# Seven products for each masked table, u ahead of the last quarter of Z, and norms in four parts

## The chip, the cores and the metric

The kernel runs on one core of one Trainium2 chip. The time is that of one execution on the device in microseconds (us). Five engines work on their own queues and meet at semaphores: TensorE (PE in the profile; PEld is its weight loads), VectorE (DVE), ScalarE (ACT), GpSimd (POOL) and SyncE (SP), which here issues all DMA transfers in one queue.

## The reference

One encoder layer is applied to two sequences, a prompt of 256 tokens and a sample of 2048, of width 1024. Half of the layer is attention in a window of a grid of 64 columns, the other half a two-dimensional Fourier transform:

```python
def encoder_layer(x, w_in, rpb, w_fourier, b_fourier, g_pre, g_na, g_f, w_out, g_post):
    h = rms_norm(x, g_pre)
    proj = h @ w_in
    q, k, v, z_a, u_f, z_f = jnp.split(proj, [...], axis=-1)     # six parts of 512
    y_a = neighbourhood_attention(q, k, v, rpb)
    y_f = fourier_mix(u_f, w_fourier, b_fourier)
    mixed = jnp.concatenate([rms_norm(y_a, g_na) * jax.nn.silu(z_a),
                             rms_norm(y_f, g_f) * jax.nn.silu(z_f)], axis=-1)
    out = mixed @ w_out
    return x + rms_norm(out, g_post)
```

The attention has 8 heads of 64. A query sees 8 rows by 16 columns of keys around it; what is outside counts as minus infinity, and a table `rpb` of relative positions is added:

```python
        logits = jnp.einsum('bjqhd,bijkhd->bhjqik', q_blk, k_slab).astype(jnp.float32) * scale
        bias = bias_table[:, row_off[None, None, :, None], col_off[:, :, None, :]]
        logits = jnp.where(valid[:, :, None, :], logits + bias, NEG_INF)
        p = jax.nn.softmax(logits.reshape(shp[:4] + (kr * K_SLAB_COLS,)), axis=-1).reshape(shp)
```

The Fourier half takes the real part of a transform over the positions and over the 64 features of each of 8 groups, and multiplies by a 512 x 512 matrix:

```python
    spec = jnp.fft.fft2(ug, axes=(1, 3), norm='ortho')
    mixed = spec.real.reshape(b, s, F_WIDTH).astype(u.dtype)
    return mixed @ w_f + b_f
```

## The kernel before, in words

Everything is in 32 bits. A product of matrices is made of three passes over operands split into a high and a low part (`mm3`, L159: lines L160 to L162 of the profile), so each operand is first copied by ACT to its high part and the rest is taken by DVE or POOL. PE's order is that of the program. In the long first part and in the last one the order of ACT, DVE, POOL and SP is that of the program too (`tc.manual_schedule(engines=MAN)`, L506 to L784 and from L1165); between L784 and L1165 a planner orders these four by its own estimates of when things are ready.

**Projections, L506 to L781.** First v and u. u goes through the first step of the Fourier transform and lies in DRAM as `ZD` (sample) and `uD` (prompt). Then the prompt's z, k and q. Then, from L686, the sample's z, k and q: 16 groups (`i`), 8 for each half of the sample's columns (`sg`), of seven products each (`j`, L722), which replace eight plain ones. One product is 12 matmuls into one of five PSUM buffers (`mmt`, L209); DVE, or ACT for the first, adds it to what it belongs to (`comb` L711, `add` L763, ACT L765), which frees the buffer. While group i is multiplied, the weights of group i+1 are combined by POOL (`w_sums`, L440) and split (`a_split`, L454 and L455), and those of group i+2 are loaded at j = 3 (`w_load`, L225). The results go to DRAM (L717, L719). The seven transformed inputs of the second half of the sample come back from DRAM through `b_get` and `b_split` (L419, L424).

**Masked tables, L479 to L503.** In the second half of the groups, and so beside these products, the bias tables of the 8 heads of the sample are masked. `t_load` (L483) takes two of 16 buffers of 8 KB per partition ("k8") and loads the raw table; `t_mask(x, 0)` puts the column mask on DVE (L489); `t_mask` with 1, 2 and 3 puts three row masks on POOL (L493), one for each kind of row; `t_store` writes two tables (L499, L500), then the third (L502). The other 14 k8 buffers hold the split inputs, so a table waits for the buffers of the one before it. The step in the code by which a table goes on is one product, and a table has six of them, from product 0 of the second half on.

**Fourier, L788 to L906.** Four quarters of `ZD` are loaded (`load_z`, L794, four transfers each) with the transform's matrices (L225), then u of the prompt (`up`, L825) and its matrix (`f256`, L823), then three more. The first two take buffers of the pool `gp`, which come free as products are done; `f256`, `up` and the rest lie in memory that the projections' pools held. For each quarter `gq` and five column blocks `c` PE makes `pab`; in the third quarter it also makes `pup` from `up` after each block (all L850). Then come the products with the Fourier weights (`ppq`, L888).

**Attention and output, from L1041.** 36 groups of a head pair and a part of the rows; iteration `k` of the loop at L1374 makes the scores of group k, the transposes and products with v of group k-1 (`transp` L1310, `pv` L1326) and half of a tile of the Fourier half's output (`f_mm`, L1256). The Fourier half's norms are sums over `sqs`, made by PE against a column of ones (`f_norm`, L1293, tile `pfn`), then a few small operations on ACT and DVE (`rsq_ops`); `f_evac(k)` needs the norm of tile k // 2. The pool of `sqs` is closed after the last of them (`pq_.close()`). The attention half has the same for its own norms (`a_norm`, L1300, tile `pna`).

Of the kernel before, what the change touches and what calls it, by code (L numbers as in the profile page):

```python
# [164 lines left out]
def build(tc, A, O):  # L165
# [54 lines left out]
    def gt(shape, dtype, name):  # L220
        return gp.tile(shape, dtype, tag="g", name=name)
# [143 lines left out]
    def n_load(x):  # L365
        if type(x) is tuple:
            nq[x] = k8(F32, "nx")
            nc.sync.dma_start(nq[x], A["xq"][0, x[0], x[1]])
            return
        nx = [k8(F32, "nx") for kh in range(2)]  # L370
        for kh in range(2):
            for b in range(2):
                nq[x, kh, b] = nx[kh][:, 2 * b:2 * b + 2]
                nc.sync.dma_start(nq[x, kh, b], A["xq"][1, kh, b][:, 2 * x:2 * x + 2])
# [55 lines left out]
    def pair(i):  # L430
        return i if i < 8 else 15 - i
# [3 lines left out]
    def w_load(i):  # L435
        wr[i] = [load(BS, A["wz"][2 * pair(i) + x], "wr") for x in range(2)]

    def w_sums(i, last=False):
        h = lambda f, k: wr[i][f][:, 4 * k:4 * k + 4]
        T2 = lambda o, i, j, op: nc.gpsimd.tensor_tensor(out=o, in0=i, in1=j, op=op)  # L440
        if last:
            T2(h(0, 1), h(0, 1), wo[i][:, 1], ALU.subtract)
            return
        wo[i] = gt([128, 2, 4, 128], F32, "ws")
        T2(wo[i][:, 0], h(1, 0), h(1, 1), ALU.add)
        T2(wo[i][:, 1], wo[i][:, 0], h(0, 0), ALU.subtract)
        T2(h(1, 0), h(0, 0), h(1, 0), ALU.subtract)
# [48 lines left out]
    def t_store(x, q):  # L496
        pr, h = divmod(x, 2)
        if q == 0:
            nc.sync.dma_start(tD[0][pr][:, h], mt[1][:, :880])  # L499
            nc.sync.dma_start(tD[2][pr][:, h], mt[1][:, 880:1840])  # L500
        else:
            nc.sync.dma_start(tD[1][pr][:, h], mt[0][:, :1200])  # L502
            mt.clear()  # L503
# [145 lines left out]
    for b in range(16):  # L649
# [25 lines left out]
        if kind % 2:  # L675
            i, d = p, o
        else:
            i = p.rearrange("p (b r c) -> p b r c", b=2, c=32)
# [7 lines left out]
    for i in range(16):  # L686
        sg, pr = divmod(i, 8)
        kind, blk = divmod(2 * pair(i), 4)
        o = [st.tile([128, 1024], F32, tag="f", name="f", bufs=3) for x in range(2)]
        uu = {}  # L690

        def e_(name):
            uu[name] = st.tile([128, 512], F32, tag="e", name=name, bufs=6)
            return uu[name]

        def dst(f, b):
            if kind % 2 == 0:
                return o[f].rearrange("p (x b c) -> p b x c", b=2, c=32)[:, b]
            if kind == 1:
                return o[f].rearrange("p (a b j) -> p b a j", b=2, j=256)[:, b]  # L700
            return o[f].rearrange("p (y b x c) -> p y x b c", y=2, b=2, c=16)[:, b]

        def src(a):
            if kind % 2 == 0:
                return a.rearrange("p (x c) -> p x c", c=32)
            if kind == 1:
                return a.rearrange("p (a j) -> p a j", j=256)
            return a.rearrange("p (x b c) -> p x b c", b=2, c=16)

        def comb(f, b, u, p, op=ALU.add):  # L710
            nc.vector.tensor_tensor(out=dst(f, b), in0=src(uu[u]), in1=src(p), op=op)  # L711

        def store(f):
            ts = slice(TP + 1024 * sg, TP + 1024 * sg + 1024)
            if kind < 2:
                silu_[0] = nc.scalar.activation(o[f], o[f], AF.Silu)
                nc.sync.dma_start(zD[kind, (blk + f) * 128:(blk + f) * 128 + 128, ts], o[f])  # L717
            else:
                nc.sync.dma_start((kD if kind == 2 else qD)[blk + f, :, ts], o[f])  # L719

        silu_ = [None]
        for j in range(7):  # L722
            if i == 7:
                aop[8, j] = aop[7, j]
            elif i < 15:
                if j == 0 and i != 8:
                    w_sums(i + 1)
                a_split(i + 1, j)
            if i == 7 and j == 1:
                w_sums(9)  # L730
            if j == 3 and i < 14 and i != 7:
                w_load(i + 2 + (i == 6))
            if sg == 0:
                x, y = divmod(7 * (pr - 1) + j, 14)
                if x in (0, 1):
                    if y == 0:
                        n_load(x)
                    elif 3 <= y < 7:
                        n_scale(x, *divmod(y - 3, 2))
                    elif 7 <= y < 12:  # L740
                        n_diff(x, y - 7)
                if pr == 6 and j in (0, 3):
                    (b_split if j else b_get)(0)
                if pr == 7 and j:
                    b_get(j)
                    if j > 2:
                        b_split(j - 2)
            if i == 8 and j < 2:
                b_split(j + 5)
            if sg:  # L750
                x, y = divmod(7 * pr + j, 6)
                if x < 8 and y == 0:
                    t_load(x)
                for q in {2: (0, 1), 3: (2,), 4: (3,)}.get(y, ()) if x < 8 else ():
                    t_mask(x, q)
                if x < 8 and y > 3:
                    t_store(x, y - 4)
            p = mmt(512)
            at = aop[i, j]
            bh, bl = bnew[sg, j]  # L760
            for k in range(4):
                mm3(nc, p, at[:, 0, k], at[:, 1, k], bh[:, k], bl[:, k], k == 0, k == 3)
            add = lambda o, u: nc.vector.tensor_tensor(out=e_(o), in0=uu[u], in1=p, op=ALU.add)  # L763
            if j == 0:
                nc.scalar.copy(e_("u0"), p)  # L765
            elif j == 1:
                comb(0, 0, "u0", p)
            elif j == 2:
                add("u2", "u0")
            elif j == 3:  # L770
                add("u4", "u2")
            elif j == 4:
                comb(1, 1, "u4", p)
                add("u3", "u2")
            elif j == 5:
                comb(1, 0, "u3", p, ALU.subtract)
                store(1)
            else:
                comb(0, 1, "u4", p)
                store(0)  # L780
        if kind < 2:  # L781
            silu = silu_[0]
# [5 lines left out]
    def load_z(gq):  # L788
        r = []
        for j in range(2):  # L790
            z = gt([128, 2, 512], F32, "zg")
            for i in range(2):
                g8 = (gq * 4 + 2 * j + i) * 8
                nc.sync.dma_start(z[:, i, :], ZD[g8:g8 + 8].rearrange("o n c -> (o n) c"))  # L794
            r += [z[:, 0, :], z[:, 1, :]]
        return r
# [4 lines left out]
    zgs = [load_z(0)]  # L801
    d2 = [load_d(0)]
    zgs.append(load_z(1))
    d2.append(load_d(1))
    zgs += [load_z(2), load_z(3)]
    ph.close()


# [14 lines left out]
    nc.sync.dma_start(f256, A["f256"])  # L823
    up = sm.tile([128, 2, 512], F32, name="up")
    nc.sync.dma_start(up, uD.rearrange("(t p) c -> p t c", p=128))  # L825
    cs2 = sm.tile([128, 2, 64], F32, name="cs2")
    nc.sync.dma_start(cs2, A["cs"])
    c32 = sm.tile([128, 4, 96], F32, name="c32")
# [461 lines left out]
    def f_norm(ts):  # L1290
        p = ps.tile([128, 18], F32, tag="c", name="pfn", bufs=1)
        for t in ts:
            nc.tensor.matmul(p[:, t:t + 1], sqs[:, t * 128:t * 128 + 128], ones, start=True, stop=True)  # L1293
        ts = slice(ts[0], ts[-1] + 1)
        rsq_ops(invf[:, ts], p[:, ts], ts.stop - ts.start, 1.0 / 512)
# [23 lines left out]
    def pv(g):  # L1319
# [28 lines left out]
        if R is None or hc:  # L1348
            nc.sync.dma_start(yD[0, pr, :, ts], y)

    WO = []

    YSQ = {2: [(Y2, 256, 512), (Y2, 512, 1024)], 3: [(Y, 256, 512), (Y2, 1024, 1664)], 4: [(Y2, 1664, 2304)],
           5: [(Y, 512, 1110)], 6: [(Y, 1110, 1708)], 7: [(Y, 1708, 2304)]}
    ftiles[0]["h"], ftiles[0]["l"] = y0h
# [18 lines left out]
    for k in range(2, len(G) + 1):  # L1374
        pr, i = divmod(k, 9)
# [17 lines left out]
        if 24 <= k < 32:  # L1393
            y = k - 24
            nc.sync.dma_start(WO[y % 2][:, y // 2].bitcast(F32), woD[0, y % 2, y // 2])
        x = k // 2 + 1
# [12 lines left out]
        if g:  # L1409
            exps(g, 0, 1)  # L1410
            bias_max(g, 1, 1)
            exps(g, 1, 0)
            f_mm(k, range(6))
            soft(g, 0)
            exps(g, 1, 1)
            if k in (4, 8):
                f_norm(range(2, 4) if k == 4 else range(4, 18))
        else:
            a_mm(atiles[0], 0, range(6))
            a_norm(atiles[:14])  # L1420
# [9 lines left out]
        run_later()  # L1430
        for v, x0, x1 in YSQ.get(k, []):
            nc.scalar.activation(v[:, x0:x1], v[:, x0:x1], AF.Square)
# [14 lines left out]
            f_evac(k)  # L1447
        if f:
            pv(f)
        if k == 8:  # L1450
            pq_.close()
        if k + 1 < len(G):
            prep_v(G[k + 1])
# [4 lines left out]
        if 32 <= k < 36:  # L1458
            x, d = k - 32, atiles[k - 32]
# [123 lines left out]
```

## Time and profile before

| | us |
|---|---|
| median of 3 runs | 1015.97 (1010.14 to 1021.81) |
| profiled execution | 1016.24 |
| its span, first to last instruction | 1014.4 |
| PE busy | 994.8 |
| DVE busy | 698.2 |
| ACT busy | 472.8 |
| POOL busy | 434.9 |

The groups of seven products run from 268 to 578 us of the span, with the tables from 424 on; the Fourier stage runs from 578 to 642, attention from there to 910, and the output's last part to the end. PE's mean granted clock is 0.990 of full speed.

In the rows of the profile "L160" is a line of the kernel, "mm<-xh,wa" the tile written and the tiles read, "x12" a count, and "[2.50 <-DMA mt<-tr]" idle time of the engine ahead of the row and what ended it. Rows of the timeline begin with the start and the duration in us. "SPq" is an issue of a DMA transfer, not the transfer. The matmuls are pipelined, so a matmul's duration is longer than the distance to the next one.

### The profile page before, as it was taken

The numbers are of one execution on the slowest core, as the hardware profiler recorded it, in microseconds if no ns is written. First come the engines' busy times: TensorE is split into PE (matmuls) and PEld (weight loads), VectorE is DVE, ScalarE is ACT, GpSimd is POOL, SyncE is SP. The second block draws the span as 40 slices with busy tenths as digits, with TensorE's granted clock in tenths as the row PEclk, the third lists the DMA queues.
The fourth block names the chain that finished last, engine by engine and source line by source line (L and its number), as shares of the span: only waits on it lengthen the run. The fifth ranks groups of instructions, "written<-read, shape, count | busy, mean of one in ns | idle before, by whom it ended". The sixth has DMA issues, their size and how long they took to land. (4 is left out here: it accounts for less than half of the span.)

```text
span 1014.4 us, 16956 instructions
## 1 busy us (share of the span) xinstructions
PE 994.8 (98%) x5828; PEld 824.7 (81%) x5828; DVE 698.2 (69%) x1287; ACT 472.8 (47%) x1022; POOL 434.9 (43%) x401
## 2 busy tenths in 40 slices
PE   7999999999999999999999999999999999999997
PEld 6778888889988888888778878878787787888886
DVE  7777637668777884896667634775565655648997
ACT  6554434256524322522123245576666676645443
POOL 2300000000526363575576113466668586633444
PEclk9999999999999999999999979999999999999999
DMA  7467798777446664866456897588678889869993
GB/s 253 140 183 221 219 322 302 265 248 242 148 170 248 233 225 171 342 215 238 168 214 231 300 327 280 195 267 265 193 248 267 277 283 289 273 222 332 345 338 131
DMA packets 153254, 249.33 MB, mean 246 GB/s; under 512 B 14033, under 2 KB 99345, under 8 KB 150609
## 3 DMA queue, kind: packets, MB, share of 16 engines
q1 hardware_dynamic: 153168, 248.26, 72.2%
q8 instruction: 46, 0.75, 0.3%
q14 instruction: 40, 0.32, 0.1%
HBM read 160.13 MB, written 88.08 MB: 245 GB/s over the span
## 5 line engine op out<-in xcount | busy, mean ns | idle before, releaser
L160 PE MATMUL mm<-xh,wa 128*128 128x512 f32 x448 | 175.3, 391 | 2.8 <-DVE u L763 2.2
L161 PE MATMUL mm<-xl,wa 128*128 128x512 f32 x448 | 175.2, 391 | 0.0
L162 PE MATMUL mm<-xh,wa 128*128 128x512 f32 x448 | 175.0, 391 | 0.0
L160 PE MATMUL mm<-wc,xh 128*128 128x512 f32 x288 | 113.7, 395 | 5.2 <-ACT xh L270 5.2
L161 PE MATMUL mm<-wc,xh 128*128 128x512 f32 x288 | 113.7, 395 | 1.1 <-DVE wc L248 1.0
L162 PE MATMUL mm<-wc,xl 128*128 128x512 f32 x288 | 113.0, 392 | 0.0
L1039 POOL TENSOR_SCALAR w<-w,m 128x480 f32<-128x480 f32 (+6 forms) x136 | 83.2, 625 | 64.1 <-DVE m L1036 52.3
L160 PEld LDWEIGHTS mm<-xh,wa 128*128 128x128 f32 x448 | 84.5, 189 | 21.2 <-issue 3.6
L161 PEld LDWEIGHTS mm<-xl,wa 128*128 128x128 f32 x448 | 84.5, 189 | 17.6
L162 PEld LDWEIGHTS mm<-xh,wa 128*128 128x128 f32 x448 | 84.6, 189 | 17.5
L1256 PE MATMUL po<-wo,yh 128*128 128x512 f32 x272 | 91.3, 417 | 0.0
L455 DVE TENSOR_TENSOR wa<-wr,wa 128x512 fp32r<-128x512 f32 x60 | 71.6, 1203 | 25.5 <-ACT wa L454 25.1
L1256 PE MATMUL po<-w,yh 128*128 128x512 f32 x280 | 86.7, 391 | 0.0
L1032 ACT ACTIVATE w<-w,m 128x480 f32<-128x480 f32 (+6 forms) x136 | 79.3, 586 | 15.3 <-DVE m L1027 15.2
L440 POOL TENSOR_TENSOR ws<-wr 128x512 f32<-128x512 f32 x15 | 22.0, 1464 | 129.5 <-DMA wr<-wz 97.2
L271 POOL TENSOR_TENSOR xl<-xr,xh 128x1024 fp32r<-128x1024 f32 x5 | 12.2, 2450 | 136.1 <-ACT xh L270 72.4
L1027 DVE CUSTOM_DVE_ANT_1 w<-s,tb 128x360 f32<-128x360 f32 (+5 forms) x124 | 62.5, 541 | 9.1 <-PE s L1005 8.5
L160 PEld LDWEIGHTS mm<-wc,xh 128*128 128x128 f32 x288 | 54.6, 189 | 16.9 <-ACT xh L270 5.2
L454 ACT CAST wa<-wr 128x512 fp32r<-128x512 f32 x60 | 36.0, 617 | 68.1 <-POOL wr L440 16.2
L493 POOL TENSOR_TENSOR mt<-mt,rmask 128x880 f32<-128x880 f32 (+2 forms) x24 | 51.1, 2138 | 37.1 <-DVE mt L489 34.6
L161 PEld LDWEIGHTS mm<-wc,xh 128*128 128x128 f32 x288 | 54.6, 190 | 14.1 <-DVE wc L248 2.8
L162 PEld LDWEIGHTS mm<-wc,xl 128*128 128x128 f32 x288 | 54.7, 190 | 11.2
(234 smaller groups left out, 2310.0 us busy)
## 6 DMA issues: line engine op xcount, KB each, us to landing
wr<-wz SPq DMA_DIRECT2D x46, 512.0 KB
oD<-ofs SPq DMA_DIRECT2D x18, 512.0 KB
of<-oD SPq DMA_DIRECT2D x18, 512.0 KB
yr<-yD SPq DMA_DIRECT2D x34, 256.0 KB
woD<-wo SPq DMA_DIRECT2D x16, 512.0 KB
zD<-f SPq DMA_DIRECT2D x16, 512.0 KB
xr<-xs SPq DMA_DIRECT2D x15, 512.0 KB
vD<-vo SPq DMA_DIRECT2D x112, 64.0 KB
```

The source lines that it names most:

```text
L160: nc.tensor.matmul(out, lh, rh, start=first, stop=False)
L161: nc.tensor.matmul(out, lh, rl, start=False, stop=False)
L162: nc.tensor.matmul(out, ll, rh, start=False, stop=last)
L271: (nc.gpsimd if c in XP else nc.vector).tensor_tensor(out=l, in0=xs[c][:, ks], in1=h.bitcast(F32), op=ALU.subtract)
L440: T2 = lambda o, i, j, op: nc.gpsimd.tensor_tensor(out=o, in0=i, in1=j, op=op)
L454: nc.scalar.copy(o[:, 0], src)
L455: nc.vector.tensor_tensor(out=o[:, 1], in0=src, in1=o[:, 0].bitcast(F32), op=ALU.subtract)
L493: nc.gpsimd.tensor_tensor(out=o, in0=i, in1=rmask[:, m0:m0 + n].unsqueeze(2).to_broadcast([128, n, 80]), op=ALU.add)
L1027: nc.vector.tensor_tensor_reduce(out=rows(g["w"][b][:, h, :n], w), in0=rows(g["s"][2 * b + h][:, :n], w), in1=tv, scale=1.0, scalar=3.0e38 ...
L1032: nc.scalar.activation(w, w, AF.Exp, bias=m[:, h:h + 1], scale=-1.0, accum_out=m[:, 2 + h:3 + h])
L1039: nc.gpsimd.tensor_scalar(w, w, m[:, 4 + h:5 + h], 1.0, ALU.mult, ALU.mult)
L1256: nc.tensor.matmul(p, (d["l"] if x == 2 else d["h"])[:, c], w(n, int(x == 1), c), start=j == 0, stop=j == 11)
```

## The change

Three things are moved. No arithmetic is added or taken away, but for two more sets of the small operations that follow a sum for the norms.

The table of the first head is now masked in group 5, in the first half, and those of the other seven heads in groups 8 to 14, one table to a group: load at j = 0, column mask and first row mask at j = 3, the others at 4 and 5, stores at 5 and 6. As the first table needs two k8 buffers in group 5, the first `b_get` and its `b_split` move from j = 0 and 3 of group 6 to j = 2 and 5. The last quarter of Z is loaded after `f256` and `up`. The norms of tiles 4 to 17, made at k = 8 in one go, are made at k = 8 (4 to 7), 10 (8 to 12) and 12 (13 to 17), and the pool of `sqs` is closed at k = 12.

```diff
@@ -739,22 +739,22 @@
-                if pr == 6 and j in (0, 3):
-                    (b_split if j else b_get)(0)
+                if pr == 6 and j in (2, 5):
+                    (b_split if j > 2 else b_get)(0)
                 if pr == 7 and j:
                     b_get(j)
                     if j > 2:
                         b_split(j - 2)
             if i == 8 and j < 2:
                 b_split(j + 5)
-            if sg:
-                x, y = divmod(7 * pr + j, 6)
-                if x < 8 and y == 0:
+            if i == 5 or 8 <= i < 15:
+                x = max(0, i - 7)
+                if j == 0:
                     t_load(x)
-                for q in {2: (0, 1), 3: (2,), 4: (3,)}.get(y, ()) if x < 8 else ():
+                for q in {3: (0, 1), 4: (2,), 5: (3,)}.get(j, ()):
                     t_mask(x, q)
-                if x < 8 and y > 3:
-                    t_store(x, y - 4)
+                if j > 4:
+                    t_store(x, j - 5)
@@ -802,7 +802,7 @@
     d2 = [load_d(0)]
     zgs.append(load_z(1))
     d2.append(load_d(1))
-    zgs += [load_z(2), load_z(3)]
+    zgs.append(load_z(2))
     ph.close()
@@ -823,6 +823,7 @@
     nc.sync.dma_start(f256, A["f256"])
     up = sm.tile([128, 2, 512], F32, name="up")
     nc.sync.dma_start(up, uD.rearrange("(t p) c -> p t c", p=128))
+    zgs.append(load_z(3))
@@ -1349,6 +1350,8 @@
+    NT = {4: range(2, 4), 8: range(4, 8), 10: range(8, 13), 12: range(13, 18)}
@@ -1413,8 +1416,8 @@
-            if k in (4, 8):
-                f_norm(range(2, 4) if k == 4 else range(4, 18))
+            if k in NT:
+                f_norm(NT[k])
@@ -1447,7 +1450,7 @@
-        if k == 8:
+        if k == 12:
             pq_.close()
```

## The prediction

> **What bounds the kernel now.** I read the engines' busy times first, then TensorE's (PE's) waits, then the granted clock in stretches, then the queues around each wait.
>
> ```profile
> PE 994.8 (98%) x5828; PEld 824.7 (81%) x5828; DVE 698.2 (69%) x1287; ACT 472.8 (47%) x1022; POOL 434.9 (43%) x401
> ```
>
> PE is the bound, so an edit pays only where PE idles or runs slow. In the waits of PE, from column two: who released it, us in total, times, longest:
>
> ```profile
> PE mm L160 <- DVE u L763: 2.2, 1, 2.2
> PE pup L850 <- DMA up<-uD: 1.9, 1, 1.9
> ...
> PE mm L160 <- DVE f L711: 0.5, 1, 0.5
> ```
>
> These three are the idle time that the change can touch: 4.6 us. The clock shows more. Busy time by stretches (length, then busy us and instructions of PE, PEld, DVE, ACT, POOL, then granted clock, DMA share, GB/s):
>
> ```profile
> 300.00:400.00 100.00, 100.00 (x443) 82.85 (x442) 75.90 (x90) 31.30 (x48) 51.95 (x30) 1.00 0.59 216
> 525.62:529.03 3.41, 3.41 (x10) 2.65 (x9) 1.78 (x2) 1.56 (x2) 3.33 (x3) 0.50 0.41 164
> 590.48:600.72 10.24, 10.24 (x77) 9.62 (x78) 2.87 (x8) 2.60 (x9) 0.00 (x0) 0.50 0.92 335
> 703.12:706.53 3.41, 3.41 (x13) 2.94 (x13) 1.45 (x6) 1.84 (x5) 1.05 (x3) 0.50 0.88 224
> 904.50:907.92 3.42, 3.42 (x28) 3.22 (x28) 0.96 (x4) 0.85 (x3) 0.00 (x0) 1.00 0.75 265
> 565.00:590.00 25.00, 23.19 (x191) 20.71 (x189) 12.88 (x33) 8.40 (x16) 0.00 (x0) 1.00 0.99 352
> 625.00:630.00 5.00, 5.00 (x31) 5.00 (x30) 2.91 (x15) 2.47 (x6) 1.84 (x3) 1.00 0.27 109
> ```
>
> Row 1 gives the pitch of the split products: 443 matmuls in 100 us, so a product of 12 takes 2.71 us and a group of 7 takes 19.0. Rows 2 to 4 are three stretches at half clock, of 3.41, 10.24 (three times 3.41) and 3.41 us. They start 64.86 and 112.64 us apart, 19 and 33 times 3.41, so the clock is judged in fixed steps of 3.41 us. Each begins where the step before it held a hole: the 2.2 us wait, the 1.9 us wait, or a burst of one-column matmuls (the norms, below). A hole costs its own length and half of the slow stretch behind it.
>
> [...]
>
> **Tables in seven products.** The first hole, on VectorE (DVE):
>
> ```profile
> 521.37 1.41 DVE L489 TENSOR_TENSOR mt<-csm,mt 128x1200 f32<-128x1200 f32 x1 [2.50 <-DMA mt<-tr]
> 522.69 0.68 DVE L711 TENSOR_TENSOR f<-u,mm 128x512 f32<-128x512 f32 x1
> 523.29 0.68 DVE L763 TENSOR_TENSOR u<-u,mm 128x512 f32<-128x512 f32 x1
> ```
>
> DVE is in order. It stands waiting for a table's load, then masks it, and only then adds the product (L763) whose PSUM buffer PE wants. PE has five such buffers, so DVE may be some 13 us late (5 x 2.71) before PE feels it; the lateness is built up by these waits, over 440 to 540 us:
>
> ```profile
> L489 DVE TENSOR_TENSOR mt<-csm,mt 128x1200 f32<-128x1200 f32 x6 | 9.5, 1591 | 15.6 <-DMA mt<-tr 15.6
> ```
>
> Six tables made DVE wait 15.6 us. The loads are late because of the in-order DMA queue of SyncE (SP):
>
> ```profile
> 494.92 0.32 SPq L502 DMA_DIRECT2D tD<-mt  x1
> 495.35 1.34 SPq L225 DMA_DIRECT2D wr<-wz  x2
> ...
> 516.24 0.37 SPq L483 DMA_DIRECT2D mt<-tr  x1
> ```
>
> A table's store (L502) waits for GpSimd (POOL); behind it stand the weight loads (L225), then the next table's load. The loop of one table is: load issued to mask 516.24 to 521.37, 5.1 us; mask on DVE 1.4; three row masks on POOL, with the weight sums (L440) in between on the same engine:
>
> ```profile
> L440 POOL TENSOR_TENSOR ws<-wr 128x512 f32<-128x512 f32 x15 | 22.0, 1464 | 129.5 <-DMA wr<-wz 97.2
> ...
> L493 POOL TENSOR_TENSOR mt<-mt,rmask 128x880 f32<-128x880 f32 (+2 forms) x24 | 51.1, 2138 | 37.1 <-DVE mt L489 34.6
> ```
>
> Masks are 3 x 2.14 = 6.4 us, sums 4 x 1.46 = 5.9. So the loop is 5.1 + 1.4 + 6.4 = 12.9 us without the sums and 18.8 with all of them inside. Before, a table has six products, 16.3 us, and its place drifts through the group, so the sums fall inside and the store blocks the weight loads. After, it has 19.0 us and fixed places: load at product 0, masks at 3, 4 and 5, stores at 5 and 6, sums at 0 and 1, weight loads at 3. The mask comes three products (8.1 us) after the load against 5.1 needed. Even the 18.8 fits. So I take this hole as gone: 2.2 + 0.5 + half of 3.41 = **4.4 us**, bounds 0 (lateness stays) and 5 (products slightly stretched around it).
>
> What is paid: the first table moves into group 5, with 1.4 us of DVE and 6.4 of POOL. There POOL is about half busy (52 of 100 us in the first row) and PE needs nothing of it, so 0; without that cover it would be 6.4. Two products later come the first reload of the transformed inputs and its split (b_get, b_split): their buffers are the table's, so SP waits at b_get until the table's last store has read out. Behind it stand weight loads with a whole group to spare. Split to first use stays nine products, 24 us. The last table ends one product later, so the Fourier loads queued behind it start later by up to 2.7 us of plan; they gain more from DVE no longer being late.
>
> **u ahead of Z's last quarter.** The second hole, PE's rows:
>
> ```profile
> 578.57 1.08 PE L850 MATMUL pab<-d,zg 128*128 128x64 f32 x8
> 579.49 0.34 PE L850 MATMUL pny<-dnyq,zg 128*128 128x1 f32 x2
> ...
> 590.13 0.88 PE L850 MATMUL pup<-f,up 128*128 128x129 f32 x4 [1.94 <-DMA up<-uD]
> 590.80 1.81 PE L850 MATMUL pab<-d,zg 128*128 128x64 f32 x8
> 592.40 1.18 PE L850 MATMUL pup<-f,up 128*128 128x129 f32 x4
> ...
> 600.52 0.72 PE L888 MATMUL ppq<-wf,cs 128*64 128x512 f32 x2
> ```
>
> Eight pab matmuls take 0.92 us at full clock (578.57 to 579.49) and 1.60 at half (590.80 to 592.40). From 590.80 to 600.52 the same work at full clock would take 9.72 x 0.92/1.60 = 5.6 us, a loss of 4.1. With the wait of 1.9 the episode costs 6.0. The queue:
>
> ```profile
> 562.65 0.32 SPq L502 DMA_DIRECT2D tD<-mt  x1
> ...
> 573.61 6.80 SPq L794 DMA_DIRECT2D zg<-ZD  x8
> 580.82 0.32 SPq L717 DMA_DIRECT2D zD<-f  x1
> 581.50 0.33 SPq L823 DMA_DIRECT2D f<-f  x1
> 582.13 0.41 SPq L825 DMA_DIRECT2D up<-uD  x1
> ```
>
> The DMA engines are full here (0.99), so a place in the queue is time. Eight loads of Z take 6.8 us, Z's last four 3.4: u landed when PE's wait ended, 590.13; with those behind it, it lands 3.4 us earlier, at 586.7, against a need at 588.2. That is thin, but all these loads begin only after the last table's store (562.65), and with DVE on time that store and the zD stores come some microseconds earlier. Z's last quarter is then late by up to 3.4 us and needed only after the whole third quarter, 5.6 us on; the stores of zD behind it have no reader here. I take **6.0 us**, bounds 0 (u late again) and 6.3.
>
> **Norms in four parts.** In PE's rows:
>
> ```profile
> 700.06 3.18 PE L1293 MATMUL pfn<-ones,sqs 128*128 128x1 f32 x28
> ...
> 903.17 3.18 PE L1300 MATMUL pna<-ones,ysq 128*128 128x1 f32 x28
> ```
>
> The same 28 matmuls now come as 8, 10 and 10, each at most 1.1 us in a step of 3.41. The sister burst for the attention half (pna, to 906.35) put 1.9 us into the step 904.50 to 907.92 and kept clock 1.00, so 1.1 won't cost it. Gain half of 3.41, 1.7. Two more starts and two more sets of small operations: no row shows them; from 0 to 0.5, nearer 0 as PE waits for none of them; I take 0.2. Net **1.5 us**, bounds -0.5 and 1.7. Keeping sqs to k = 12 costs nothing, as no allocation claims it before k = 23.
>
> That sister burst is not changed, but its place against the steps is. A slow step followed 1.9 us of wait and 3.1 us of norms (the step 699.71 to 703.12), not 1.9 us of norms; so somewhere between these lies the border, and by where a burst of 3.2 us falls in 3.41 it costs 1.7 us in 1 to 8 of 10 cases. I add half, **0.9**.
>
> Sum, against the profiled execution's 1016.24 (0.3 above the median of 1015.97): 1016.24 - 4.4 - 6.0 - 1.5 + 0.9 = **1005.2**.
>
> **The rivals.**
> *Tables still late* (chance 0.11): DVE keeps waiting because loads take longer than the 5.1 us I used. 1016.24 - 6.0 - 1.5 + 0.9 = 1009.6. Against it: 8.1 us are given.
> *u still late* (0.13): its buffer lies in memory that the products' operands hold to the end, so SP takes Z's last quarter first after all and the move does nothing. 1016.24 - 4.4 - 1.5 + 0.9 = 1011.2; if the wait goes but the small matmuls hold the clock down, 1009.3.
> *The clock is not the holes'* (0.03): slow steps come from something else and stay, and only the waits are saved, 1016.24 - 4.6 = 1011.6. [...] Three slow stretches of three behind a hole speak against it.
> *Given back later* (0.08): PE arrives 10 us earlier than loads that haven't moved, 1014 to 1016. Against it: by 625 us the DMA share has fallen to 0.27, so the pile is worked off while PE still has no need of it.
> *Slower* (0.03): a table loop longer than a group. With excess e per table, seven tables make DVE 7e late, 13 of it hidden; PE then waits 7e - 13, and the time passes 1016 from e = 3.4, a loop of 22.4 us. At e = 5 it is 1005 + 22 = 1027. The rows give 18.8 at most.
>
> **How the numbers follow.** The forecast has 0.62. The runs before lie between 1010.14 and 1021.81, so single runs move by some us. The likeliest case's own range is 1001 to 1008: 2 us either way for the unchanged burst and the bounds of the parts, more for the spread. The range for all, 1000.5 to 1012, takes in the first three rivals and leaves out giving back and slower. One per cent, about what a measurement here can tell from no change, is 10.2 us, so the border is 1005.8, just above the forecast. Of the 0.62, 0.47 falls below it, and 0.02 of the rest; that makes faster 0.49. Slower by over 1%, past 1026, are the slower rival's 0.03 and 0.02 of stray runs of the others, 0.05; the rest, 0.46, ends within 1%.
>
> **What would show it.** Right: no wait of DVE at L489 beyond 1 us, no PE wait on L763 or L711 between 400 and 580 us; pup without a wait and clock 1.00 through the Fourier stage; pfn in bursts of 8, 10 and 10 with no 0.50 after them. Wrong: up issued behind all sixteen loads of Z; a 10.24 us slow stretch without a hole before it; new PE waits on wr, kl or wo.

## The result and the profile after

The changed kernel takes 1004.24 us (median of 6 runs, 1003.07 to 1006.0), beside 1017.13 us for the kernel before on the same chip (median of 6 runs, 1010.14 to 1021.81): a ratio of 0.9876, 95% interval 0.984 to 0.9912. The forecast was 1005.2 us in a range of 1000.5 to 1012. The profiled execution took 1003.15 us, with a span of 1001.2 us.

Engines' busy times of the changed kernel, and PE's waits (who released it, us in total, times, longest):

```profile
PE 987.3 (99%) x5828; PEld 819.9 (82%) x5828; DVE 688.2 (69%) x1295; ACT 474.4 (47%) x1026; POOL 438.3 (44%) x401
...
PE mm L160 <- ACT xh L270: 5.2, 1, 5.2
```

Before, the span of 1014.4 had 994.8 of busy PE, so 19.6 us idle. Now it has 987.3 of 1001.2, so 13.9. Of the 13.2 us gone from the span, 5.7 are idle time and 7.5 are the same 5828 matmuls running faster. The three waits that the change could touch, 4.6 us, are all gone; the one above lies at the start of the kernel, and the others that are left are 0.3 us or less. The stretches of the changed kernel that answer to those shown of before (columns as there; the granted clock stands behind the five engines):

```profile
430.00:530.00 100.00, 100.00 (x443) 82.87 (x442) 72.73 (x86) 26.37 (x44) 68.68 (x39) 1.00 0.61 222
...
564.50:600.00 35.50, 35.50 (x326) 28.77 (x325) 17.11 (x46) 15.81 (x37) 7.49 (x6) 1.00 0.90 317
...
891.51:894.93 3.42, 3.42 (x13) 2.70 (x12) 1.16 (x5) 0.97 (x3) 0.00 (x0) 0.50 0.22 85
```

PE is busy without a gap at full clock through the second half of the groups and the Fourier stage. Between the start and the last microseconds only one stretch at half clock is left, 3.41 us long, where there were 3.41, 10.24 and 3.41. It is new: it stands behind the attention half's burst of norms, which the change left alone. Half of the 13.65 us of half clock that went is 6.8, most of the 7.5 above.

The groups of the tables' column mask on DVE, in 430 to 560 us of the changed kernel:

```profile
L489 DVE TENSOR_TENSOR mt<-csm,mt 128x1200 f32<-128x1200 f32 x7 | 9.8, 1400 | 0.0
```

Seven tables, and no idle time of DVE ahead of them, where six had 15.6 us. The queue of SP behind them, in the changed kernel:

```profile
533.46 0.37 SPq L502 DMA_DIRECT2D tD<-mt  x1
...
552.50 0.37 SPq L502 DMA_DIRECT2D tD<-mt  x1
...
561.24 5.07 SPq L794 DMA_DIRECT2D zg<-ZD  x6
...
572.40 0.45 SPq L825 DMA_DIRECT2D up<-uD  x1
...
574.21 1.51 SPq L794 DMA_DIRECT2D zg<-ZD  x2
```

The last table's store goes out at 552.50 instead of 562.65, although its plan ends one product later, and u's load at 572.40 instead of 582.13. Only two loads of Z come behind u, not the four of the last quarter. PE in the Fourier stage, and the projection norms:

```profile
582.33 0.67 PE L851 MATMUL pup<-f,up 128*128 128x129 f32 x4
...
588.11 1.94 PE L889 MATMUL ppq<-wf,cs 128*64 128x512 f32 x8
...
701.35 1.17 PE L1294 MATMUL pfn<-ones,sqs 128*128 128x1 f32 x10
...
716.26 1.17 PE L1294 MATMUL pfn<-ones,sqs 128*128 128x1 f32 x10
...
888.38 3.18 PE L1301 MATMUL pna<-ones,ysq 128*128 128x1 f32 x28
```

From the first product with u to the first with the next matrices PE needs 5.8 us (582.33 to 588.11). Before it was 12.3, from 588.19, where its wait for u began (590.13 less 1.94), to 600.52.

The same two profiled runs by stages, each from the start of its first matmul in PE's timeline (267.91, 577.54, 611.82 and 903.17 us before; 267.16, 571.83, 599.33 and 888.38 now):

| stage | before, us | now, us | gone, us |
|---|---|---|---|
| up to the sample's 16 groups | 267.91 | 267.16 | 0.75 |
| the groups, to the first `pab` | 309.63 | 304.67 | 4.96 |
| Fourier, to the first `py` (the products after `ppq`) | 34.28 | 27.50 | 6.78 |
| from there to the attention half's burst (`pna`, x28) | 291.35 | 289.05 | 2.30 |
| from there to the end | 111.24 | 112.83 | -1.59 |

The 0.75 us lie ahead of all that was changed. So the total came out in the range, and every slow place named was gone. What these views can't tell is which of the three edits removed which place.

### The profile page after: what moved, and what is told of

Read it like the earlier page. It is cut to its first block, busy times and chain, and to the rows that moved or that the text cites. A ratio compares the mean times of both kernels' runs of the same rounds, so it can differ in the third digit from the quotient of the medians.

```text
span 1001.2 us, 16950 instructions
## 1 busy us (share of the span) xinstructions
PE 987.3 (99%) x5828; PEld 819.9 (82%) x5828; DVE 688.2 (69%) x1295; ACT 474.4 (47%) x1026; POOL 438.3 (44%) x401
## 4 chain that ended last, share of the span: by engine, by line
PE 94%; DVE 2%; DMA 1%; ACT 1%; issue 1%; SPq 0%; POOL 0%; DVEq 0%; ACTq 0%; POOLq 0%
PE po L1257 19%; PE mm L161 17%; PE mm L160 17%; PE mm L162 17%; PE pv L1327 6%; PE ptb L1311 6%; PE s L1006 4%; PE pab L851 2%; DMA wr<-wv 1%; PE py L160 1%; PE py L162 1%; PE py L161 1%; DVE wc L248 1%; DVE sq L279 1%; PE pz L161 0%
## 5 line engine op out<-in xcount | busy, mean ns | idle before, releaser
L1033 ACT ACTIVATE w<-w,m 128x480 f32<-128x480 f32 (+6 forms) x136 | 79.3, 586 | 14.5 <-DVE m L1028 14.5
L455 DVE TENSOR_TENSOR wa<-wr,wa 128x512 fp32r<-128x512 f32 x60 | 63.0, 1057 | 30.0 <-ACT wa L454 29.7
L440 POOL TENSOR_TENSOR ws<-wr 128x512 f32<-128x512 f32 x15 | 24.3, 1622 | 119.2 <-DMA wr<-wz 97.8
L711 DVE TENSOR_TENSOR f<-u,mm 128x512 f32<-128x512 f32 x64 | 43.6, 682 | 32.0 <-PE mm L162 22.3
L161 PEld LDWEIGHTS mm<-wc,xh 128*128 128x128 f32 x288 | 54.8, 190 | 13.2 <-DVE wc L248 1.7
```

Of the source, the lines that this page charges most:

```text
L161: nc.tensor.matmul(out, lh, rl, start=False, stop=False)
L455: nc.vector.tensor_tensor(out=o[:, 1], in0=src, in1=o[:, 0].bitcast(F32), op=ALU.subtract)
L1033: nc.scalar.activation(w, w, AF.Exp, bias=m[:, h:h + 1], scale=-1.0, accum_out=m[:, 2 + h:3 + h])
```

## The experiments

Two theories stood after the result. By A, the prediction's, each edit earns its own term: the tables 4.4, u's place 6.0, the norms 1.5. By B the tables carry u's term too: with DVE on time, every transfer behind the last table goes out earlier, and u's place in the queue doesn't matter.

### Which edit earns what

*The tables alone* (the kernel before with the hunks of the tables and `b_get`):

```diff
+            if i == 5 or 8 <= i < 15:
+                x = max(0, i - 7)
+                if j == 0:
                     t_load(x)
...
```

> The kernel before with the tables in seven products alone (and the first b_get and b_split two products later). Theory A, each part earns its own term as in the sum of the prediction: the tables' 4.4 us alone, so 4.4 us under the kernel before (about 1012.7 against 1017.1), with PE's wait for up of 1.9 us and its slow stretch of 10.24 us still there. Theory B, the tables carry u's term too, because VectorE on time lets the zD stores and with them all loads of Z and u go out earlier: no wait for up, and 4.4 + 6.0 = 10.4 us under the kernel before (about 1006.7); only the norms' burst is left with its slow step.

1004.57 us (1002.43 to 1007.16), ratio 0.9855, interval 0.9804 to 0.9907: as much as the whole change. PE doesn't wait for u. SP's queue of this kernel:

```profile
571.61 1.20 SPq L794 DMA_DIRECT2D zg<-ZD  x2
574.71 0.80 SPq L825 DMA_DIRECT2D up<-uD  x1
```

u goes out behind all sixteen loads of Z, as in the old order, and is still on time, because the queue got there 7.4 us earlier than before (574.71 against 582.13). PE reads it at 582.35.

*u's place alone* (the kernel before with the two lines on `load_z(3)`):

```diff
-    zgs += [load_z(2), load_z(3)]
+    zgs.append(load_z(2))
...
+    zgs.append(load_z(3))
```

> The kernel before with u and its matrix written ahead of Z's last quarter alone. Theory A: 6.0 us under the kernel before (about 1011), no wait for up, clock 1.00 in the Fourier stage. Theory B, the planner keeps its order, since the memory of f256 and up is held until the last product while Z's buffers are free earlier: no change (within 2 us of 1017), up is issued behind all sixteen loads of Z and PE waits for it again.

1018.9 us (1011.44 to 1023.82, 10 runs), ratio 1.0003, interval 0.9976 to 1.003: nothing. Its waits of PE, and the last of SP's loads, in the profiled run, which was the fastest of the ten:

```profile
PE mm L160 <- DVE u L763: 2.5, 1, 2.5
PE pup L851 <- DMA up<-uD: 1.2, 1, 1.2
PE mm L160 <- DVE f L711: 0.6, 1, 0.6
...
574.40 6.60 SPq L794 DMA_DIRECT2D zg<-ZD  x8
582.71 0.44 SPq L825 DMA_DIRECT2D up<-uD  x1
```

The program names u first, but SP still issues the eight loads of Z ahead of it. That is the order which the prediction's rival *u still late* forecast. Its reason, that u's memory is held by the products' operands to the end, is not shown by a run. PE waits for u here too, 1.2 us; what that means for the clock is told further down.

*The change without u's place* (the two lines put back):

> The changed kernel with Z's last quarter back ahead of u; tables and norms as changed. Theory A: u's 6.0 us are lost, 1010 against 1004.2. Theory B: up is issued some 2 us later than in the changed kernel, where it landed at 577.1 and was needed at 582.3, so it lands by 580 and nothing changes: within 1 us of 1004.2, no wait for up, no slow step in the Fourier stage.

1003.79 us (1003.13 to 1005.85), ratio 0.985, interval 0.9801 to 0.9899; there is no wait for u. Both sides agree: u's place earns nothing alone, and beside the tables nothing that these runs can tell. A's division falls, B's holds.

### The norms and the clock

*The change with the projection norms in one burst:*

```diff
-    NT = {4: range(2, 4), 8: range(4, 8), 10: range(8, 13), 12: range(13, 18)}
+    NT = {4: range(2, 4), 8: range(4, 18)}
...
-        if k == 12:
+        if k == 8:
```

> The changed kernel with the norms of tiles 4 to 17 in one burst at k = 8 again. Theory A: where the burst falls so that one step of 3.41 us holds 3 us of it, a slow step follows and the kernel is 1.5 us slower (1005.7); where it is cut near its middle by a step's border, as the attention half's burst was before, no slow step follows and it is 0 to 0.3 us faster. Rival: the time of the norms is that of their small operations, not of the clock; then one burst is faster by the two sets of operations saved, wherever it falls.

1006.28 us in the median of four widely spread runs (1003.14 to 1009.71), ratio 0.9872, interval 0.9815 to 0.9929. The profiled run, the slowest of the four, has 6.83 us at half clock behind this burst and 6.83 behind the attention half's:

```profile
691.04:697.87 6.83, 6.83 (x32) 5.35 (x31) 2.20 (x7) 1.84 (x5) 3.09 (x4) 0.50 0.87 276
895.84:902.67 6.83, 6.83 (x35) 5.67 (x36) 1.16 (x5) 0.97 (x3) 0.00 (x0) 0.50 0.19 71
```

So a burst can cost two slow steps as well as one. But the kernel with the tables alone, which has the old burst too, reached 1004.57; the parts of the norms are worth between 0.3 and 2.0 us by these medians, which the runs don't separate from nothing.

The traces say more. From the first `py` to the attention half's burst, the kernels with four parts profiled here (the changed one, the one without u's place, the two with holes told of below, and the four of the section after this one) take 289.0 to 289.9 us. With one burst it is 289.8 where no slow step follows it (u's place alone), 291.3 behind one slow step (the kernel before, the tables alone) and 292.9 behind two (this kernel). So four parts cost nothing that can be seen, and one slow step went with about 1.5 us more.

*The change with the attention norms in three parts as well:*

```diff
+            if k in (32, 34):
+                a_norm(atiles[:6] if k == 32 else atiles[6:10])
         else:
             a_mm(atiles[0], 0, range(6))
-            a_norm(atiles[:14])
+            a_norm(atiles[10:14])
```

> The changed kernel with the attention half's norms of tiles 0 to 13 in three parts too: tiles 0 to 5 at k = 32, 6 to 9 at k = 34, 10 to 13 at k = 36. The burst of 3.2 us is the only one left that a slow step followed, of 3.41 or 6.83 us (in the changed kernel 3.41, in two of the experiments 6.83, in the kernel before none). Clock theory: the slow step goes, 1.7 to 3.4 us in the executions that had one, so the median falls by about 2 to near 1002.3, and the runs lie closer together. Rival, the bursts cost by their number: two more starts and two more sets of small operations, the same or 0.5 us slower.

1002.54 us (1001.66 to 1003.78, 6 runs), ratio 0.9845, interval 0.9811 to 0.9879: the best version of all, 1.7 us under the change in the median, about half of a slow step of 3.41. The intervals of the two overlap. The stretch in its profile around that burst:

```profile
880.00:960.00 80.00, 80.00 (x436) 66.02 (x435) 65.42 (x142) 36.98 (x106) 32.33 (x31) 1.00 0.89 308
```

No slow step is left between the start and the last microseconds of this kernel.

*How large must a hole be?* Two kernels have holes of known length put into the changed one: after product 0 of each group PE runs one added small matmul, which waits for none to three added copies on ACT, chained one after another; the second kernel has the copies in another order, so that the holes fall at other places. That work is extra, so their total times say nothing of the change.

```diff
+    HOLES = (0, 1, 2, 3) * 4          # in the second kernel: (3, 2, 1, 2) * 4
...
+                for x in range(HOLES[i]):
+                    nc.scalar.copy(uu["u0"], uu["u0"])
+                hole = ps.tile([128, 64], F32, tag="c", name="hole", bufs=1)
+                nc.tensor.matmul(hole, onesq, uu["u0"][:, :64], start=True, stop=True)
```

> The changed kernel with holes put into PE's work to measure what a hole costs. After product 0 of each group, ScalarE copies the finished product onto itself 0, 1, 2 or 3 more times (groups 0 to 15 in turn), and a small matmul that reads it makes PE wait: four holes each of about 1.0, 1.5, 2.1 and 2.7 us. Clock theory: holes whose part within one step of 3.41 us is 1.9 us or more are followed by a slow step, those of 1.2 us or less by none, the border lies between; with random places, none of the 1.0, most of the 2.7. [...]

> [...]

They took 1059.92 and 1066.11 us, in one run each. The granted clock changes on a grid of 3.413 us in both; 60 such steps also lie between the slow stretches of the kernel with one burst (691.04 and 895.84). Four steps of this grid in the second kernel, each step with a hole followed by the next one; PE's busy time is short of 3.41 by the hole:

```profile
435.16:438.57 3.41, 1.63 (x8) 1.41 (x9) 0.00 (x0) 1.67 (x3) 0.00 (x0) 1.00 0.82 245
438.57:441.99 3.42, 3.42 (x10) 2.67 (x9) 0.42 (x1) 0.47 (x1) 0.00 (x0) 0.50 0.90 381
459.05:462.46 3.41, 1.70 (x8) 1.46 (x9) 3.41 (x2) 3.35 (x5) 2.29 (x1) 1.00 0.81 289
462.46:465.88 3.42, 3.42 (x16) 2.81 (x15) 2.84 (x2) 1.62 (x3) 1.30 (x1) 1.00 0.26 40
```

With 1.78 us of hole in a step, the next step is at half clock. With 1.70 us (3.41 less the busy time, before rounding) it isn't, although that hole is the longer one, 2.62 us against 1.97, since 0.92 of it lie in the step before. Over the holes of both kernels the largest share of a step that passed was 1.70 and the smallest that did not was 1.76, 0.50 and 0.52 of a step. So in these two kernels it wasn't the length of a hole that decided, but how much of one step of the grid it filled.

### What in the tables' edit earns it

The edit has two halves: the first table in group 5, and seven products for each. The prediction costed the first at nothing and gave the gain to the second. In the next three kernels the first `b_get` and its `b_split` stand at their old places.

*The change without the early table* (eight tables of seven products, groups 8 to 15):

```diff
...
-            if i == 5 or 8 <= i < 15:
-                x = max(0, i - 7)
+            if sg:
+                x = i - 8
```

> The changed kernel with the first head's table not in group 5: eight tables of seven products in groups 8 to 15 (and the first b_get and b_split at their old places). Tests what the early first table is for. If it is only room in GpSimd's time, nothing changes within 1 us. If it is the place of the last store against the loads of Z and u: the last table's store falls into group 15 (its mask ends some 17 us into it), the last eight loads of Z, f256 and up come behind it, up lands within 1 us of its need, and PE waits for Z or u up to 2 us, with a slow stretch behind it in some executions: 0 to 6 us slower than the changed kernel, and runs further apart.

1018.78 us (1016.5 to 1019.93, 10 runs), ratio to the kernel before 1.0002, interval 0.998 to 1.0025: the whole gain is lost. The waits of PE (first) and the timeline of DVE and of PE in this kernel, then one stretch of it:

```profile
PE pab L851 <- DVE abl L844: 3.5, 1, 3.5
...
577.63 0.42 DVE L843 CAST abh<-pab 128x256 fp32r<-128x256 f32 x1 [4.73 <-DMA tD<-mt]
...
578.93 1.94 PE L851 MATMUL pab<-d,zg 128*128 128x64 f32 x8 [3.51 <-DVE abl L844]
...
577.11:604.42 27.31, 25.49 (x184) 23.37 (x186) 9.16 (x31) 5.91 (x19) 0.00 (x0) 0.50 0.94 333
```

The last table's store goes out with the last products. DVE's first step of the Fourier stage writes to memory that this table held, and waits 4.73 us for the store to read it out; PE, whose PSUM buffers DVE has to empty, stops for 3.5 us, and the Fourier stage's small matmuls run at half clock for 27.31 us, eight steps in a row, the first of which holds the end of the stop. From the first `pab` (572.01) to the first `py` (614.74) the stage takes 42.7 us against 27.5 in the change: 15.2 of the 16.0 us between the two profiled runs, 3.5 of them the stop. u is not the cause: PE waits for it nowhere here. Nor is DVE late: ahead of the eight column masks it has 0.1 us of idle time (430 to 575 us), and PE has no wait on L763 or L711. So seven products remove the first hole without the early table, and the late end of the tables alone loses as much as the whole edit gains.

*The early table with six products for the others*, in two places: where they stood before the change, and starting with group 8, so that the last ends with group 13.

```diff
-            if i == 5 or 8 <= i < 15:
-                x = max(0, i - 7)
+            if i == 5 or sg:
+                x, y = (0, j) if i == 5 else divmod(7 * pr + j + 0, 6)     # in the second kernel: + 6
...
-                for q in {3: (0, 1), 4: (2,), 5: (3,)}.get(j, ()):
+                for q in {2: (0, 1), 3: (2,), 4: (3,)}.get(y, ()) if (i == 5 or 0 < x < 8) else ():
...
```

> The changed kernel with the first head's table in group 5 as there, but every table in six products again: tables two to eight stand where they stood before the change, and the last ends with the sixth product of group 14, as before. It asks which half of the tables' edit earns the 13 us: the seven products, or the first table's early place.
> By the prediction's theory (the loop of a table, up to 18.8 us, doesn't fit six products, 16.3 us): DVE waits at L489 as before, some 1.5 to 2.5 us per table, its lateness grows to 10 us or more, PE stops once around 525 us for 1 to 2 us and a slow step of 3.41 us follows it, and the last store goes out late, so that u is late again: 1011 to 1017 us.
> By the rival (the early first table is what matters, as its absence cost 14.5 us): no long slow stretch in the Fourier stage, 1003 to 1007 us, with or without waits at L489.

> As the kernel with the six-product tables and the early first one, but tables two to eight begin with group 8 and follow each other without a gap, so that the last ends with group 13, a whole group (19 us) ahead of the changed kernel's last.
> By the theory of the seven products: DVE's waits at L489 come back and PE stops once for 1 to 2 us with a slow step behind it (3 to 4 us in all), but the Fourier stage's loads are no longer behind a late table, so no slow stretch there: 1006 to 1010 us.
> By the rival of the early end (whatever ends the tables early enough does the same): 1003 to 1006 us.

The first took 1012.56 us (1008.58 to 1014.64, 10 runs), ratio 0.9948, interval 0.9925 to 0.9971; the second 1009.34 (1008.84 to 1011.08, 10 runs), ratio 0.9935, interval 0.9905 to 0.9964. Waits of PE and the group of DVE's column masks (430 to 560 us) of the first, then the same of the second:

```profile
PE pup L851 <- DMA up<-uD: 2.5, 1, 2.5
PE mm L160 <- DVE f L711: 0.5, 1, 0.5
...
L489 DVE TENSOR_TENSOR mt<-csm,mt 128x1200 f32<-128x1200 f32 x7 | 9.8, 1406 | 11.8 <-DMA mt<-tr 11.8
```

```profile
PE mm L160 <- DVE u L763: 2.6, 1, 2.6
PE mm L160 <- DVE f L711: 0.6, 1, 0.6
...
L489 DVE TENSOR_TENSOR mt<-csm,mt 128x1200 f32<-128x1200 f32 x7 | 10.9, 1563 | 16.7 <-issue 10.8 <-DMA mt<-tr 6.0
```

Each keeps one of the two holes of the kernel before. In the first, DVE's idle time ahead of the tables is 11.8 us, all of it for their loads, instead of 16.3 in the same window of the kernel before; the hole at 525 us that the theory expected has shrunk to 0.5 us without a slow step, so the theory missed there. But the last store is still late (560.23 against 552.50 in the change), u too, and 10.24 us at half clock follow. In the second the tables end early enough for u, but DVE is late, the hole at 524 us is there, and 3.41 us at half clock. Of its 16.7 us of idle time only 6.0 are put to the loads; for 10.8 the profile shows no releaser. Of the places tried, only seven products with an end in group 14, for which the first table has to start early, remove both holes. The prediction's account of the loop (too long for six products, short enough for seven) stands.

*Seven products in another place of the group* (the change with tables two to eight shifted by three products: load at 3, masks at 6 and at 0 and 1 of the next group, stores ahead of its weight loads):

```diff
-            if i == 5 or 8 <= i < 15:
-                x = max(0, i - 7)
+            n = i * 7 + j if i < 8 else i * 7 + j - 3
+            if 35 <= n < 42 or 56 <= n < 105:
+                x, y = max(0, n // 7 - 7), n % 7
...
```

> The changed kernel with tables two to eight shifted by three products: seven products each, but the load goes out at product 3, the masks fall at product 6 and at products 0 and 1 of the next group, beside the weight sums, and the stores stand ahead of that group's weight loads. The last table ends three products (8.1 us) later, with product 2 of group 15. It tells the period from the place in the group.
> By the theory that the fixed place away from the sums matters: DVE waits at L489 1 to 2 us per table again, it is 3 to 5 us late, PE isn't stopped in groups 8 to 14; what the later end costs comes on top, 1004 to 1009 us.
> By the theory that only the period matters: no waits at L489; 1004 us if the 8.1 us of a later end are hidden, and 1009 to 1018 us with u late and a slow stretch in the Fourier stage if they aren't.

1031.68 us (1029.98 to 1034.16), ratio 1.0147, interval 1.0101 to 1.0194: slower than the kernel before, and worse than either theory gave. PE's wait, DVE's group (430 to 575 us), and then the queue of SP in this kernel:

```profile
PE mm L160 <- DVE f L711: 7.6, 4, 2.5
...
L489 DVE TENSOR_TENSOR mt<-csm,mt 128x1200 f32<-128x1200 f32 x7 | 9.8, 1407 | 25.4 <-DMA mt<-tr 25.4
```

```profile
520.99 0.32 SPq L502 DMA_DIRECT2D tD<-mt  x1
521.42 1.33 SPq L225 DMA_DIRECT2D wr<-wz  x2
522.84 0.41 SPq L483 DMA_DIRECT2D mt<-tr  x1
...
543.57 0.32 SPq L502 DMA_DIRECT2D tD<-mt  x1
543.99 1.34 SPq L225 DMA_DIRECT2D wr<-wz  x2
545.42 0.41 SPq L483 DMA_DIRECT2D mt<-tr  x1
```

From load to load a table takes 22.6 us here (522.84 to 545.42), in a group of 19.0. POOL's rows, where the masks now mix with the weight sums, of this kernel and then of the change:

```profile
508.60 1.66 POOL L493 TENSOR_TENSOR mt<-mt,rmask 128x880 f32<-128x880 f32 x1 [10.59 <-DVE mt L489]
510.22 1.72 POOL L440 TENSOR_TENSOR ws<-wr 128x512 f32<-128x512 f32 x1
...
518.77 2.19 POOL L493 TENSOR_TENSOR mt<-mt,rmask 128x1200 f32<-128x1200 f32 x1
```

```profile
525.75 6.70 POOL L493 TENSOR_TENSOR mt<-mt,rmask 128x880 f32<-128x880 f32 x3 [4.87 <-DVE mt L489]
532.41 1.29 POOL L440 TENSOR_TENSOR ws<-wr 128x512 f32<-128x512 f32 x1
```

Three masks take 12.4 us (508.60 to 520.96) with the sums between them and 6.70 without. The store waits for the last mask, the weight loads and the next table's load stand behind the store, and the circle closes a product and more too late in each group. Theory and rival of this run both missed: it isn't the period alone, and the price of a bad place was put at 3 to 5 us of lateness that PE wouldn't feel, but it is some 3.6 us per table, which adds up and stops PE four times. It is the slower rival of the prediction, brought about: a loop of more than 22.4 us. The Fourier stage has 27.31 us at half clock here too, behind a wait of 2.0 us for the transform's matrix, whose load stands behind the last store. Of the 26.8 us between the profiled runs of this kernel and the change, the groups take 11.7 and the wait and the Fourier stage 14.6; so the second part is again the price of the tables' late end, to which the plan's 8.1 us and the growing lateness both add.

## Why the prediction was right, and where it was not

**The bound.** Right: PE is the bound, and waits and slow steps were what there was to win. The three waits (4.6 us) and 13.65 us of half clock went. The forecast took 11.0 us from the profiled run before, and the profiled runs differ by 13.1.

**Tables in seven products, 4.4.** The groups became 5.0 us shorter. The mechanism is confirmed from both sides: seven products at these places leave DVE no idle time ahead of the tables, with the early table and without it; six products bring DVE's waits back, in both kernels with six, though they stopped PE noticeably in only one; and a table that meets the weight sums brings a loop of 22.6 us. The places in the group count as much as the number. But two statements in this part missed something. "PE needs nothing of it, so 0" was right as a price of the first table's new place and missed what the place earns: without it the whole edit is worth nothing. And the last table's later end was set at "up to 2.7 us of plan" against gains from an on-time DVE. The balance came out right, but an end one group later costs 14.5 us in the median, through memory that the Fourier stage reuses; no step looked at who takes the tables' buffers after them.

**u ahead of Z's last quarter, 6.0.** The failed step. The wait of 1.9 and the slow 10.24 us are gone, and the Fourier stage is 6.8 us shorter, but the edit that the term was written under earns nothing. What was said there in passing, "with DVE on time that store and the zD stores come some microseconds earlier", is the cause, together with the early first table, which lets the last one end in group 14: u's load moved up 7.4 us by the tables alone. The rival *u still late* had SP's order right where u's place is changed alone, and the time wrong, because it left the tables' effect on this queue out; its 1011.2 would have needed the old lateness. The two terms shared a queue and were not independent. That the sum came out was luck in this part: one edit carried both terms. The size was a little low because the pace was read between unlike rows: 0.92 us is the pace of eight `pab` beside `pny`. In the changed kernel eight `pab` between two `pup`, as in the slow stretch, take 0.84 (582.83 to 583.67) against the 1.60, so a slow stretch there costs nearly half of its length.

**Norms in four parts, 1.5.** The bursts of 8, 10 and 10 ran at full clock with no slow step behind them, as forecast, in every kernel that has them. Their stage is 2.3 us shorter in the profiled change and 1.4 to 1.8 us shorter in the other kernels with four parts, against the two with one slow step. In the medians the gain isn't shown: 0.3 to 2.0 us by the two comparisons. The 0.2 us set against it for two more starts and sets of small operations was the author's estimate, and no run shows it by itself.

**The unchanged burst, 0.9.** It was given half a chance of a slow step, which was too little: a slow stretch followed it in 11 of the 12 profiles in which it is one burst, 3.41 us long in six of them and 6.83 in five; only the kernel before had none. The change pays 1.6 us for it, and splitting that burst too gains 1.7 in the median. With the 0.75 us ahead of the groups, the measured terms are 0.75 + 4.96 + 6.78 + 2.30 - 1.59 = 13.2 us of the span, where the forecast had 4.4 + 6.0 + 1.5 - 0.9 = 11.0: in this pair of runs each gain was put too low, and so was the one cost.

**The clock.** In every profile the half-clock stretches ahead of the end are 3.41 us long or a whole number of times that (6.83, 10.24 and 27.31 us: two, three and eight). The border that the prediction left open "somewhere between" was measured at two values. For plain holes among the large products it lay at 1.70 to 1.76 us in one step, in the two kernels with holes. For the bursts of 28 one-column matmuls it lay at 2.03 to 2.14 us of the burst in one step: 2.03 passed with u's place alone (695.16 to 698.34, a step beginning at 696.31), 2.14 did not with the tables alone (890.62 on, the slow stretch from 892.76). The waits of the kernel before, 1.91 and 1.94 us within one step in its profile, lie just above the first border. The kernel with u's place alone had a wait of 1.2 us for u and no slow stretch there, and its profiled run was its fastest, 1011.44. That may be why the kernel before spreads over 11.7 us and the changed one over 2.9. The runs fit that: of all those of the kernel before that stand beside the experiments, the four below 1012 us have a mean granted clock of 0.995 or 0.996, and those from 1020 to 1025 have 0.983 to 0.989. Why a run gets more or fewer slow steps wasn't tested by itself.

**Given back later, slower.** Neither came: there are no new waits behind 600 us, and the table loop fits its group.

## What to carry to other kernels

Before an edit is given a gain, ask which other edit moves the same queue: leave each one out and take each one alone, since a queue that runs on time can make another edit's gain its own, as u's load, 7.4 us earlier by the tables alone, did here. When work is spread over a period, count what meets it on each in-order engine at that place; the same period with another offset was 27 us apart, some 12 of them in the groups themselves and the rest through the late end. And look at who gets the buffers of the last round of a stage: a stage that ended late was paid for here in the next one's first write: DVE waited 4.73 us, and the Fourier stage took 15.2 us more.

## What the runs showed of the hardware

Among the large products of the two kernels with holes, a step at half clock followed each step of the 3.413 us grid in which PE was idle for 1.76 us or more, and none with 1.70 or less. A hole shorter than a step was enough in the kernel before too: PE's wait of 2.24 us that ended at 524.12, 1.91 of it in one step, was followed by 3.41 us at half clock from 525.62. In the Fourier stage of the kernel without the early table, 1.69 us were enough, in a step that otherwise held small matmuls (the stop begins at 575.42, the slow stretch at 577.11). The grid didn't follow the holes: in the second kernel with holes the slow steps behind single holes begin at 394.20, 438.57, 482.95 and 527.32 us, 13 steps of 3.413 us apart each time, while the holes ahead of them lie 44.0 to 45.4 us apart.

Bursts of one-column matmuls acted like holes, though the profile counts PE as busy throughout (3.41 of 3.41 us in the step 699.71 to 703.12 of the kernel before, ahead of its slow step). Behind 14 of the 16 unsplit bursts of 28 (3.18 us at full clock) in these profiles a slow step followed; behind the bursts of 8, 10 and 12 (0.95 to 1.40 us) none did.

In these runs small matmuls didn't bring the clock back soon. Behind a single hole among the large products the clock was back after one step; in the Fourier stage, with PE busy, but for the end of one stop, on matmuls of 64 and 129 columns, it stayed at half for 10.24 us (the kernel before, and the one with the early table and six products) and for 27.31 us (without the early table, and with the shifted ones). So a hole of about the same length was followed by three to eight slow steps there and by one among the products. In all four kernels the clock came back within 1.8 us of the start of the first products of 512 columns (`ppq`): at 600.72 with `ppq` from 600.52 (before), 597.23 with 597.52, 604.42 with 602.67 and 614.62 with 614.48. By which property of the matmuls it recovers wasn't tried.
